# Index add: one plain transfer queue in a hand-written order, and gathers without repeated rows

## The chip, the cores and the metric

The kernel runs on one core of a Trainium2 chip. The core has a TensorE for matrix products (PE in the profile, its weight loads PEld), VectorE (DVE), ScalarE (ACT), GpSimd (POOL) and SyncE (SP), each with its own instruction stream, and 16 DMA engines that move data between the device memory and the core's SBUF. SP and ACT issue plain transfers here, each on a queue of its own; GpSimd issues the indirect ones, whose rows are given by a list of row numbers. The metric is the time of one execution on the device in microseconds; lower is better.

## The reference

`x` holds 32 batches of 512 rows of 256 floats (16.8 MB). For every batch there are 128 row numbers and 128 source rows, and each source row is added to the row of the result that its number names. Numbers can repeat within a batch, and then all their source rows are added.

```python
batch, seq, dim = 32, 512, 256
num_updates = 128
...
result = x.copy()
for b in range(batch):
    for i in range(num_updates):
        result[b, indices[b, i]] += source[b, i]
```

The inputs are the same at each execution. Each batch has between 107 and 119 distinct numbers among its 128.

## The kernel before

The 32 batches are handled in two ways.

Batches 0 to 25 (`NB` of them) go by rows. A plain transfer copies the whole batch of 512 KB from `x` to `out` (L119). A gather (L278) fetches the 128 rows of `x` that the batch's numbers name into SBUF. In `scatter` (L288) PE multiplies a 128x128 matrix of zeros and ones, which says which updates of the batch share a row, with the source rows; DVE adds the gathered rows (`res`, L299); and an indirect transfer writes the sums to `out` (L302). The scatter of a batch must come after its copy, since it overwrites rows of it. Where a number repeats, every update of that row holds the same complete sum, and only the first is written: `target` holds the row number, raised by `ROWS` for every later repeat, and the scatter's bound drops rows past `ROWS - 1`.

The matrix and `target` come from `equality` (L185), for four batches at a time: small matmuls spread the row numbers (L191), and DVE compares (`eq`, L199), masks (`early`, L206), reduces (`again`, L210) and forms `target` (L218). Groups are formed inside the loop, at its every fourth step.

Batches 26 to 31 (`N_FULL` of them) go whole: a plain transfer loads 512 KB into SBUF (L96), `compute_full` (L230) adds the source rows by matmuls with one-hot matrices (L243, L250), and a plain transfer stores the result (L259).

What sets the order: SP issues the index load and then the 26 copies, in order. ACT issues the 8 source loads of four batches each (L86) interleaved with the six whole loads, then the whole stores, the first three in the loop and the last three at its end (`STORES_LAST`). GpSimd's order is written out by hand with `pool_next`: five gathers ahead (`AHEAD`), then gather `b + 5` and scatter `b` in turn. On DVE and PE a scheduler places the instructions. It also gives each transfer its completion semaphore, and it derives the waits from the tiles. `ordered` declares which writes to `out` need no order among them, and ties each scatter to its copy.

Of the kernel before, what the change touches and what calls it, by code (L numbers as in the profile page):

```python
# [8 lines left out]

G = 4  # L10
N_FULL = 6
AHEAD = 5
COPY_RUN = 8192
FULL_AT = {1: 0, 4: 1, 8: 2, 12: 3, 16: 4, 20: 5}
STORES_LAST = 3


@with_exitstack
def kernel(
# [7 lines left out]
    nc = tc.nc  # L27

    B, S, D = x.shape
    _, NU = indices.shape  # L30
    assert NU == P and B % G == 0 and S % P == 0
    NG = B // G
    ROWS = B * S
    CH = S // P
    NB = B - N_FULL
# [11 lines left out]
    spool = ctx.enter_context(tc.tile_pool(name="spool", bufs=NG))  # L47
    xpool = ctx.enter_context(tc.tile_pool(name="xpool", bufs=N_FULL))
    hpool = ctx.enter_context(tc.tile_pool(name="hpool", bufs=2))
    epool = ctx.enter_context(tc.tile_pool(name="epool", bufs=3))  # L50
    mpool = ctx.enter_context(tc.tile_pool(name="mpool", bufs=2))
    gpool = ctx.enter_context(tc.tile_pool(name="gpool", bufs=AHEAD + 3))
    rpool = ctx.enter_context(tc.tile_pool(name="rpool", bufs=8))
    bpsum = ctx.enter_context(tc.tile_pool(name="bpsum", bufs=2, space=PSUM))
    apsum = ctx.enter_context(tc.tile_pool(name="apsum", bufs=3, space=PSUM))
# [3 lines left out]
    x_rows = x.rearrange("b s d -> (b s) d")  # L59
# [6 lines left out]

    writes = []

    def ordered(ins, after=()):
        for other in writes:  # L70
            if not any(other is a for a in after):
                tc.declare_no_dep(ins.ins, other.ins, reason="other rows")
        for a in after:
            tc.add_manual_dep(ins.ins, a.ins.name, SYNC, reason="the same rows")
        writes.append(ins)
        return ins


    idx_raw = const.tile([B, NU * 2], i32)
    nc.sync.dma_start(out=idx_raw[:, :], in_=indices.bitcast(i32))  # L80

    src = {}

    def load_src(g):
        t = spool.tile([P, G, D], f32, tag="src")
        nc.scalar.dma_start(  # L86
            out=t[:, :, :],
            in_=source[g * G : (g + 1) * G].rearrange("e u d -> u e d"),
        )
        src[g] = t  # L90

    full = {}

    def load_full(b):
        t = xpool.tile([P, CH, D], f32, tag="full")
        nc.scalar.dma_start(  # L96
            out=t[:, :, :], in_=x[b].rearrange("(j c) d -> j c d", c=CH)
        )
        full[b] = t

    load_src(0)
    load_full(NB)
    load_src(NB // G)
    load_full(NB + 1)
    load_src(1)
    g_next = 2
    for b in range(NB + 2, B):
        if b // G not in src:
            load_src(b // G)
        load_full(b)  # L110
        if g_next not in src:
            load_src(g_next)
        g_next += 1
    for g in range(NG):
        if g not in src:
            load_src(g)

    copies = [
        ordered(nc.sync.dma_start(out=out[b], in_=x[b], max_dma_last_dim=COPY_RUN))  # L119
        for b in range(NB)  # L120
    ]


    ident = const.tile([B, B], f32)
# [2 lines left out]
        out=ident[:, :],  # L127
        in_=ident[:, :],
# [13 lines left out]
        out=lower[:, :, :],  # L142
        in_=lower[:, :, :],
# [15 lines left out]
        out=idx_bt[:, :],  # L159
        in_=idx_raw[:, :].rearrange("b (u w) -> b u w", w=2)[:, :, 0],  # L160
# [5 lines left out]
    row_i = const.tile([P, B], i32)  # L166
    nc.vector.tensor_tensor(  # L167
        out=row_i[:, :], in0=base_i[:, :], in1=idx_f[:, :], op=Alu.add
# [3 lines left out]
        out=row_f[:, :], in0=base_i[:, :], in1=idx_f[:, :], op=Alu.add  # L172
# [10 lines left out]
    eqs, targets = {}, {}  # L183

    def equality(g):  # L185
        n = min(G, NB - g * G)
        sl = slice(g * G, g * G + n)
        rep = bpsum.tile([P, G, P], f32, tag="rep")
        for e in range(n):
            b = g * G + e  # L190
            nc.tensor.matmul(  # L191
                out=rep[:, e, :],
                lhsT=ident_h[:, b : b + 1].to_broadcast([B, P]),
                rhs=idx_h[:, :],
                start=True,
                stop=True,
            )
        eq = epool.tile([P, G, P], f32, tag="eq")
        nc.vector.tensor_tensor(  # L199
            out=eq[:, :n, :],  # L200
            in0=rep[:, :n, :],
            in1=idx_f[:, sl].unsqueeze(2).to_broadcast([P, n, P]),
            op=Alu.is_equal,
        )
        early = mpool.tile([P, G, P], f32, tag="early")
        nc.vector.tensor_tensor(  # L206
            out=early[:, :n, :], in0=eq[:, :n, :], in1=lower[:, :n, :], op=Alu.mult
        )
        again = mpool.tile([P, G], f32, tag="again")
        nc.vector.tensor_reduce(  # L210
            out=again[:, :n],
            in_=early[:, :n, :],
            axis=mybir.AxisListType.X,
            op=Alu.max,
        )

        target = epool.tile([P, G], i32, tag="target")
        nc.vector.scalar_tensor_tensor(  # L218
            out=target[:, :n],
            in0=again[:, :n],  # L220
            scalar=float(ROWS),
            in1=row_f[:, sl],
            op0=Alu.mult,
            op1=Alu.add,
        )
        eqs[g] = eq
        targets[g] = target


    def compute_full(b):  # L230
        x_tile = full[b]
        onehot = hpool.tile([P, CH, P], f32, tag="onehot")
        nc.vector.tensor_scalar(  # L233
            out=onehot[:, :, :],
            in0=line_f[:, :, :],
            scalar1=idx_f[:, b : b + 1],
            scalar2=None,
            op0=Alu.is_equal,
        )
        for c0 in range(0, CH, 2):  # L240
            ps = fpsum.tile([P, 2, D], f32, tag="ps")
            for k in range(2):
                nc.tensor.matmul(  # L243
                    out=ps[:, k, :],
                    lhsT=onehot[:, c0 + k, :],
                    rhs=src[b // G][:, b % G, :],
                    start=True,
                    stop=True,
                )
            nc.vector.tensor_tensor(  # L250
                out=x_tile[:, c0 : c0 + 2, :],
                in0=x_tile[:, c0 : c0 + 2, :],
                in1=ps[:, :, :],
                op=Alu.add,
            )

    def store_full(b):
        ordered(
            nc.scalar.dma_start(  # L259
                out=out[b].rearrange("(j c) d -> j c d", c=CH), in_=full[b][:, :, :]  # L260
            )
        )


    rows = {}
    on_pool, last_gather = [], [None]
# [1 line left out]
    def pool_next(ins):  # L268

        if on_pool:  # L270
            tc.add_manual_dep(
                ins.ins, on_pool[-1].ins.name, NOSYNC, reason="Pool's order"
            )
        on_pool.append(ins)

    def gather(b):
        t = gpool.tile([P, D], f32, tag="row")
        ins = nc.gpsimd.indirect_dma_start(  # L278
            out=t[:, :],
            out_offset=None,  # L280
            in_=x_rows,
            in_offset=bass.IndirectOffsetOnAxis(ap=row_i[:, b : b + 1], axis=0),
        )
        rows[b] = t
        last_gather[0] = ins
        pool_next(ins)

    def scatter(b):  # L288
        g, e = divmod(b, G)
        acc = apsum.tile([P, D], f32, tag="acc")  # L290
        nc.tensor.matmul(  # L291
            out=acc[:, :],
            lhsT=eqs[g][:, e, :],
            rhs=src[g][:, e, :],
            start=True,
            stop=True,
        )
        res = rpool.tile([P, D], f32, tag="res")
        nc.vector.tensor_tensor(  # L299
            out=res[:, :], in0=acc[:, :], in1=rows.pop(b)[:, :], op=Alu.add  # L300
        )
        ins = nc.gpsimd.indirect_dma_start(  # L302
            out=out_rows,
            out_offset=bass.IndirectOffsetOnAxis(ap=targets[g][:, e : e + 1], axis=0),
            in_=res[:, :],
            in_offset=None,
            bounds_check=ROWS - 1,
            oob_is_err=False,
        )
        ordered(ins, [copies[b]])  # L310
        if on_pool[-1] is last_gather[0]:
            pool_next(ins)

    for b in range(AHEAD):
        gather(b)
    for b in range(NB):
        if b + AHEAD < NB:
            gather(b + AHEAD)
        if b % G == 0:
            equality(b // G)  # L320
        scatter(b)
        if b in FULL_AT:
            compute_full(NB + FULL_AT[b])
            if FULL_AT[b] < N_FULL - STORES_LAST:
                store_full(NB + FULL_AT[b])
    for b in range(B - STORES_LAST, B):
        store_full(b)


# [28 lines left out]
```

## Time and profile before

| | us |
|---|---|
| median of three runs | 91.35 |
| the three runs | 90.51, 91.35, 92.36 |
| the profiled execution's own time | 91.25 |
| its span, first to last instruction | 89.5 |
| GpSimd busy | 54.2 |
| PE busy | 41.6 |
| DVE busy | 34.6 |

Busy time says how long an engine's instructions ran, not whether the kernel waited for them. The profile lists the DMA queues apart: for each one its packets, its bytes, and the time that the packets took as a share of the 16 engines' span. A strip gives the bytes per second in 40 equal slices of the span. Where the profile names what an idle engine waited for, the name is inferred from semaphore events; a wait for several things is put down to the one that came last by the profile.

### The profile page before, as it was taken

How to read it: one execution, taken by the hardware profiler on the slowest of the kernel's cores; microseconds unless marked ns; L12 is line 12 of the kernel's file. 1: busy time of each engine (PE TensorE's matmuls, PEld its weight loads, DVE VectorE, ACT ScalarE, POOL GpSimd, SP SyncE). 2: the span in 40 equal slices, each digit the busy share in tenths (PEclk: the TensorE clock that was granted, in tenths of full speed). 3: DMA queues.
4: the chain of work that ended last, by engine and by line, in shares of the span. 5: the costliest groups of instructions: out<-in, count | busy, mean ns of one | idle time of the engine just before them, and what ended most of it. 6: DMA issues, size and time to landing. Idle time of an engine off the chain costs nothing.

```text
span 89.5 us, 597 instructions
## 1 busy us (share of the span) xinstructions
PE 41.6 (46%) x127; PEld 26.2 (29%) x127; DVE 34.6 (39%) x79; POOL 54.2 (61%) x62
## 2 busy tenths in 40 slices
PE   0383008999649926893593550513557105500000
PEld 0260006767436803561381330210225002200000
DVE  0395020479746155934949191110113011022000
POOL 7277787647774317350058777877877787787500
PEclk9999999999985999669669995555555555555555
DMA  1999999999999999999999999899998999963210
GB/s 19 336 404 381 416 416 377 348 409 389 398 396 378 430 378 408 378 424 414 423 421 419 398 346 300 314 408 430 412 367 326 376 401 374 383 242 128 68 36 0
DMA packets 10579, 30.61 MB, mean 342 GB/s; under 512 B 1584, under 2 KB 5721, under 8 KB 8912
## 3 DMA queue, kind: packets, MB, share of 16 engines
q1 hardware_dynamic: 2128, 13.67, 39.0%
q10 hardware_dynamic: 5952, 10.49, 31.5%
q0 software_dynamic: 2496, 6.42, 19.5%
q8 instruction: 1, 0.02, 0.1%
q14 instruction: 2, 0.02, 0.0%
HBM read 24.41 MB, written 20.19 MB: 498 GB/s over the span
## 4 chain that ended last, share of the span: by engine, by line
DMA 50%; POOL 19%; issue 15%; POOLq 5%; DVE 3%; SPq 1%; PE 0%; DVEq 0%
DMA t<-in_x_dram,row_i 23%; DMA out_dram<-t 16%; POOL out_dram L302 11%; DMA out_dram<-in_x_dram 8%; POOL t L278 8%; POOLq L302 3%; DMA idx_raw<-in_indices_dram 3%; POOLq L353 1%; DVE t L250 1%; SPq L119 1%; DVE eq L199 1%; PE idx_ps L163 0%; DVE idx_bt L158 0%; DVE idx_f L165 0%; DVE row_i L167 0%
## 5 line engine op out<-in xcount | busy, mean ns | idle before, releaser
L302 POOL DMA_INDIRECT out_dram<-res,target x26 | 26.6, 1023 | 20.0 <-issue 8.3
L291 PE MATMUL acc<-t,eq 128*128 128x256 f32 x52 | 23.5, 576 | 23.2 <-DVE res L299 12.1
L278 POOL DMA_INDIRECT t<-in_x_dram,row_i x26 | 25.4, 978 | 9.5 <-issue 7.0
L299 DVE TENSOR_TENSOR res<-acc,t 128x256 f32<-128x256 f32 x26 | 10.9, 423 | 35.9 <-DMA t<-in_x_dram,row_i 26.5
L291 PEld LDWEIGHTS acc<-t,eq 128*128 128x128 f32 x52 | 12.4, 270 | 31.6 <-DVE res L299 14.7
L243 PE MATMUL ps<-t,onehot 128*128 128x256 f32 x48 | 16.2, 494 | 8.8 <-issue 6.3
L243 PEld LDWEIGHTS ps<-t,onehot 128*128 128x128 f32 x48 | 11.7, 255 | 13.1 <-issue 10.9
L250 DVE TENSOR_TENSOR t<-t,ps 128x512 f32<-128x512 f32 x12 | 8.1, 682 | 4.2 <-issue 3.2
L199 DVE TENSOR_TENSOR eq<-rep,idx_f 128x512 f32<-128x512 f32 (+1 forms) x7 | 4.5, 645 | 0.1
L206 DVE TENSOR_TENSOR early<-eq,lower 128x512 f32<-128x512 f32 (+1 forms) x7 | 4.5, 646 | 0.0
L210 DVE TENSOR_REDUCE again<-early 128x4 f32<-128x512 f32 (+1 forms) x7 | 4.5, 640 | 0.0
L191 PE MATMUL rep<-idx_h,ident_h 32*128 32x128 f16 x26 | 3.1, 258 | 0.0
L233 DVE TENSOR_SCALAR onehot<-line_f,idx_f 128x512 f32<-128x512 f32 x6 | 2.9, 486 | 0.0
L191 PEld LDWEIGHTS <-ident_h 32*128 32x128 f16 x26 | 1.9, 111 | 2.1 <-issue 2.0
L218 DVE SCALAR_TENSOR_TENSOR target<-again,row_f 128x4 int32<-128x4 f32 (+1 forms) x7 | 1.1, 154 | 3.5 <-issue 2.0
L163 PE MATMUL idx_ps<-ident,idx_bt 32*128 32x32 f32 x1 | 0.3, 281 | 3.8 <-DVE idx_bt L158 3.8
L158 DVE CAST idx_bt<-idx_raw 32x128 f32<-32x128 int32 x1 | 0.2, 215 | 3.4 <-DMA idx_raw<-in_indices_dram 3.4
L163 PEld LDWEIGHTS idx_ps<-ident,idx_bt 32*128 32x128 f32 x1 | 0.2, 176 | 3.7 <-POOL lower L141 3.7
L141 POOL TENSOR_SCALAR_AFFINE_SELECT lower<-lower 128x512 f32<-128x512 f32 x1 | 0.6, 627 | 0.0
L152 POOL IOTA line_i<- 128x512 int32 x1 | 0.6, 559 | 0.0
L140 POOL MEMSET lower<- 128x512 f32 x1 | 0.5, 515 | 0.0
L181 DVE CAST line_f<-line_i 128x512 f32<-128x512 int32 x1 | 0.4, 418 | 0.0
(12 smaller groups left out, 1.8 us busy)
## 6 DMA issues: line engine op xcount, KB each, us to landing
out_dram<-in_x_dram SPq DMA_DIRECT2D x26, 512.0 KB
t<-in_source_dram ACTq DMA_DIRECT2D x8, 512.0 KB
t<-in_x_dram ACTq DMA_DIRECT2D x6, 512.0 KB
out_dram<-t ACTq DMA_DIRECT2D x6, 512.0 KB
t<-in_x_dram,row_i POOLq DMA_INDIRECT x26
out_dram<-res,target POOLq DMA_INDIRECT x26
idx_raw<-in_indices_dram SPq DMA_DIRECT2D x1, 32.0 KB
```

Of the source, the lines that this page charges most:

```text
L191: nc.tensor.matmul(out=rep[:, e, :], lhsT=ident_h[:, b : b + 1].to_broadcast([B, P]), rhs=idx_h[:, :], start=True, stop=True,)
L199: nc.vector.tensor_tensor(out=eq[:, :n, :], in0=rep[:, :n, :], in1=idx_f[:, sl].unsqueeze(2).to_broadcast([P, n, P]), op=Alu.is_equal,)
L206: nc.vector.tensor_tensor(out=early[:, :n, :], in0=eq[:, :n, :], in1=lower[:, :n, :], op=Alu.mult)
L210: nc.vector.tensor_reduce(out=again[:, :n], in_=early[:, :n, :], axis=mybir.AxisListType.X, op=Alu.max,)
L218: nc.vector.scalar_tensor_tensor(out=target[:, :n], in0=again[:, :n], scalar=float(ROWS), in1=row_f[:, sl], op0=Alu.mult, op1=Alu.add,)
L233: nc.vector.tensor_scalar(out=onehot[:, :, :], in0=line_f[:, :, :], scalar1=idx_f[:, b : b + 1], scalar2=None, op0=Alu.is_equal,)
L243: nc.tensor.matmul(out=ps[:, k, :], lhsT=onehot[:, c0 + k, :], rhs=src[b // G][:, b % G, :], start=True, stop=True,)
L250: nc.vector.tensor_tensor(out=x_tile[:, c0 : c0 + 2, :], in0=x_tile[:, c0 : c0 + 2, :], in1=ps[:, :, :], op=Alu.add,)
L278: ins = nc.gpsimd.indirect_dma_start(out=t[:, :], out_offset=None, in_=x_rows, in_offset=bass.IndirectOffsetOnAxis(ap=row_i[:, b : b + 1], ...
L291: nc.tensor.matmul(out=acc[:, :], lhsT=eqs[g][:, e, :], rhs=src[g][:, e, :], start=True, stop=True,)
L299: nc.vector.tensor_tensor(out=res[:, :], in0=acc[:, :], in1=rows.pop(b)[:, :], op=Alu.add)
L302: ins = nc.gpsimd.indirect_dma_start(out=out_rows, out_offset=bass.IndirectOffsetOnAxis(ap=targets[g][:, e : e + 1], axis=0), in_=res[:, : ...
```

## The change

All plain transfers are issued by SP. Their order is a table: `s` is a source load, `f` a whole load, `c` a copy, `w` a whole store, and the entries of a step are issued ahead of the step's gather and scatter. Ahead of the loop stand `s0 c0 c1 s1 c2`; five of the six whole stores stand behind the loop. The whole batches are computed in the order 28, 29, 30, 31, 26, 27, at other steps than before. Gathers run four ahead instead of five. The first eight gathers read all 128 rows; from batch 8 on, a gather takes its row numbers from `target` with a bound, so that it leaves out the repeated rows. Their places in the tile keep older data, and the scatter drops the same places. For that, `equality` runs two groups ahead, and its tiles have four buffers instead of three. The tiles of the gathers have eight buffers as before. `ordered` no longer declares that a plain write is independent of another plain write, only pairs with an indirect one.

```diff
-AHEAD = 5
+AHEAD = 4
+RAW = 8
...
-FULL_AT = {1: 0, 4: 1, 8: 2, 12: 3, 16: 4, 20: 5}
-STORES_LAST = 3
+PLAN = {
+    0: "c3 s7 f28 c4",
+    1: "s2 c5",
+    2: "c6 f29",
+    3: "c7",
+    4: "c8 s3",
+    5: "c9 f30",
+    6: "c10",
+    7: "c11",
+    8: "s4 c12",
+    9: "c13 f31",
+    10: "c14",
+    11: "c15 s5",
+    12: "c16",
+    13: "c17 s6",
+    14: "c18 f26",
+    15: "c19 w28",
+    16: "c20",
+    17: "c21 f27",
+    18: "c22",
+    19: "c23",
+    20: "c24 c25",
+}
+LAST = "w29 w30 w31 w26 w27"
+FULL_AT = {3: 28, 6: 29, 9: 30, 13: 31, 18: 26, 21: 27}
...
-    epool = ctx.enter_context(tc.tile_pool(name="epool", bufs=3))
+    epool = ctx.enter_context(tc.tile_pool(name="epool", bufs=4))
...
+    def transfers(plan):
+        for what in plan.split():
+            kind, n = what[0], int(what[1:])
+            {"s": load_src, "f": load_full, "c": copy, "w": store_full}[kind](n)
...
     def gather(b):
         t = gpool.tile([P, D], f32, tag="row")
+        if b < RAW:
...
+        else:
+            g, e = divmod(b, G)
+            ins = nc.gpsimd.indirect_dma_start(
+                out=t[:, :],
+                out_offset=None,
+                in_=x_rows,
+                in_offset=bass.IndirectOffsetOnAxis(
+                    ap=targets[g][:, e : e + 1], axis=0
+                ),
+                bounds_check=ROWS - 1,
+                oob_is_err=False,
+            )
...
+    transfers("s0 c0 c1 s1 c2")
+    equality(0)
+    equality(1)
     for b in range(AHEAD):
         gather(b)
     for b in range(NB):
+        if b in PLAN:
+            transfers(PLAN[b])
         if b + AHEAD < NB:
             gather(b + AHEAD)
-        if b % G == 0:
-            equality(b // G)
+        if b % G == 0 and (b // G + 2) * G < NB:
+            equality(b // G + 2)
         scatter(b)
         if b in FULL_AT:
-            compute_full(NB + FULL_AT[b])
-            if FULL_AT[b] < N_FULL - STORES_LAST:
-                store_full(NB + FULL_AT[b])
-    for b in range(B - STORES_LAST, B):
-        store_full(b)
+            compute_full(FULL_AT[b])
+    transfers(LAST)
```

`load_src`, `load_full` and `store_full` issue with `nc.sync` instead of `nc.scalar`; nothing else in them changes, and `copy` is the former list of copies, one at a time.

More of the change, by code (lines that the diff above doesn't have):

```diff
@@ L49 @@
     hpool = ctx.enter_context(tc.tile_pool(name="hpool", bufs=2))
-    epool = ctx.enter_context(tc.tile_pool(name="epool", bufs=3))
+    epool = ctx.enter_context(tc.tile_pool(name="epool", bufs=4))
     mpool = ctx.enter_context(tc.tile_pool(name="mpool", bufs=2))
-    gpool = ctx.enter_context(tc.tile_pool(name="gpool", bufs=AHEAD + 3))
+    gpool = ctx.enter_context(tc.tile_pool(name="gpool", bufs=RAW))
     rpool = ctx.enter_context(tc.tile_pool(name="rpool", bufs=8))
@@ L67, with ordered @@
     writes = []
-    def ordered(ins, after=()):
-        for other in writes:
-            if not any(other is a for a in after):
+    def ordered(ins, after=(), indexed=False):
+        for other, other_indexed in writes:
+            if (indexed or other_indexed) and not any(other is a for a in after):
                 tc.declare_no_dep(ins.ins, other.ins, reason="other rows")
@@ L74, in ordered @@
             tc.add_manual_dep(ins.ins, a.ins.name, SYNC, reason="the same rows")
-        writes.append(ins)
+        writes.append((ins, indexed))
         return ins
@@ L80 @@
     nc.sync.dma_start(out=idx_raw[:, :], in_=indices.bitcast(i32))
-    src = {}
+    src, full, copies = {}, {}, {}
     def load_src(g):
         t = spool.tile([P, G, D], f32, tag="src")
-        nc.scalar.dma_start(
+        nc.sync.dma_start(
             out=t[:, :, :],
@@ L90, in load_src @@
         src[g] = t
-    full = {}
     def load_full(b):
         t = xpool.tile([P, CH, D], f32, tag="full")
-        nc.scalar.dma_start(
+        nc.sync.dma_start(
             out=t[:, :, :], in_=x[b].rearrange("(j c) d -> j c d", c=CH)
@@ L99, in load_full, with copy, store_full @@
         full[b] = t
[L101 to L121, printed above, removed]
+    def copy(b):
+        copies[b] = ordered(
+            nc.sync.dma_start(out=out[b], in_=x[b], max_dma_last_dim=COPY_RUN)
+        )
+    def store_full(b):
+        ordered(
+            nc.sync.dma_start(
+                out=out[b].rearrange("(j c) d -> j c d", c=CH), in_=full[b][:, :, :]
+            )
+        )
+    def transfers(plan):
+        for what in plan.split():
+            kind, n = what[0], int(what[1:])
+            {"s": load_src, "f": load_full, "c": copy, "w": store_full}[kind](n)
     ident = const.tile([B, B], f32)
@@ L255, in compute_full @@
             )
[L257 to L262, printed above, removed]
     rows = {}
@@ L277, in gather @@
         t = gpool.tile([P, D], f32, tag="row")
[L278 to L283, printed above, removed]
+        if b < RAW:
[3 more added lines that the diff above has]
+                in_=x_rows,
+                in_offset=bass.IndirectOffsetOnAxis(ap=row_i[:, b : b + 1], axis=0),
+            )
+        else:
+            g, e = divmod(b, G)
+            ins = nc.gpsimd.indirect_dma_start(
+                out=t[:, :],
+                out_offset=None,
+                in_=x_rows,
+                in_offset=bass.IndirectOffsetOnAxis(
[3 more added lines that the diff above has]
+                oob_is_err=False,
+            )
         rows[b] = t
@@ L309, in scatter @@
         )
-        ordered(ins, [copies[b]])
+        ordered(ins, [copies[b]], indexed=True)
         if on_pool[-1] is last_gather[0]:
             pool_next(ins)
+    transfers("s0 c0 c1 s1 c2")
+    equality(0)
+    equality(1)
     for b in range(AHEAD):
```

## The prediction

> **What bounds the kernel now.** I read the page's slices and queues first, then stages, then GpSimd's own order of work, then SP's waits.
>
> ```profile
> span 89.5 us, 597 instructions
> ...
> GB/s 19 336 404 381 416 416 377 348 409 389 398 396 378 430 378 408 378 424 414 423 421 419 398 346 300 314 408 430 412 367 326 376 401 374 383 242 128 68 36 0
> DMA packets 10579, 30.61 MB, mean 342 GB/s; under 512 B 1584, under 2 KB 5721, under 8 KB 8912
> ## 3 DMA queue, kind: packets, MB, share of 16 engines
> q1 hardware_dynamic: 2128, 13.67, 39.0%
> q10 hardware_dynamic: 5952, 10.49, 31.5%
> q0 software_dynamic: 2496, 6.42, 19.5%
> ...
> HBM read 24.41 MB, written 20.19 MB: 498 GB/s over the span
> ```
>
> q1 is SP's queue (copies), q10 ACT's (sources, whole loads and stores), q0 GpSimd's (gathers, scatters). Together they keep 16 DMA engines busy for 39.0 + 31.5 + 19.5 = 90% of 89.5, 80.6 us. No compute engine is near that. The idle tenth lies at the two ends, as the stages show (columns: busy us of PE, PEld, DVE, POOL, clock, DMA share, GB/s):
>
> ```profile
> 0.00:5.00 5.00, 1.23 (x9) 0.94 (x9) 1.34 (x7) 2.42 (x11) 1.00 0.60 202
> ...
> 80.00:85.00 5.00, 0.00 (x0) 0.00 (x0) 0.85 (x2) 3.52 (x4) 0.50 0.28 98
> 85.00:89.50 4.50, 0.00 (x0) 0.00 (x0) 0.00 (x0) 0.00 (x0) 0.50 0.08 26
> ```
>
> After 80 the DMA engines have 0.28 and then 0.08 of their time filled, yet the kernel isn't done. GpSimd is why. Its timeline (start, duration, operation, idle time before):
>
> ```profile
> 4.80 1.12 POOL L278 DMA_INDIRECT t<-in_x_dram,row_i  x1 [1.93 <-DVE row_f L171]
> ...
> 12.49 1.03 POOL L302 DMA_INDIRECT out_dram<-res,target  x1 [0.30 <-issue]
> ...
> 33.33 1.02 POOL L302 DMA_INDIRECT out_dram<-res,target  x1 [3.34 <-DVE res L299]
> 34.65 0.98 POOL L278 DMA_INDIRECT t<-in_x_dram,row_i  x1 [0.30 <-issue]
> 37.29 1.02 POOL L302 DMA_INDIRECT out_dram<-res,target  x1 [1.67 <-DVE onehot L233]
> 38.62 0.98 POOL L278 DMA_INDIRECT t<-in_x_dram,row_i  x1 [0.30 <-issue]
> 45.41 1.02 POOL L302 DMA_INDIRECT out_dram<-res,target  x1 [5.82 <-DVE eq L199]
> ...
> 83.45 0.99 POOL L302 DMA_INDIRECT out_dram<-res,target  x1 [0.30 <-issue]
> ```
>
> The scatter at 45.41 is number 8. From there GpSimd has 29 more indirect transfers to start and starts them without a gap: (83.45 - 45.41) / 29 = 1.31 us a slot. So everything after 45 is fixed by when scatter 8 could start; the engine named beside its 5.82 us had long been done, so I look for a transfer. SP's own waits tell which:
>
> ```profile
> SPq L119 <- DMA out_dram<-t: 8.3, 1, 8.3
> SPq L119 <- DMA t<-in_source_dram: 8.0, 3, 3.1
> ...
> SPq L119 <- DMA t<-in_x_dram: 1.0, 1, 1.0
> ```
>
> L119 issues copies, which need nothing from a source, a whole load or a store; still SP waits 17.3 us for such transfers to land before it may issue the next copy. I infer that plain transfers of both queues share a few completion semaphores, so a copy waits for an older transfer of ACT's. Copies come late, scatter 8 with them, and GpSimd pays at the end.
>
> **The change part by part.**
>
> *One plain queue.* 8 + 6 loads and 6 stores move from ACT to SP; ACT issues nothing.
>
> ```profile
> L86 ACTq DMA_DIRECT2D t<-in_source_dram x8: 374/413/1292, 0.8 to 27.7; - x8
> L96 ACTq DMA_DIRECT2D t<-in_x_dram x6: 529/1214/3782, 1.3 to 22.9; - x6
> L259 ACTq DMA_DIRECT2D out_dram<-t x6: 338/347/1542, 28.1 to 53.7; - x6
> ...
> L119 SPq DMA_DIRECT2D out_dram<-in_x_dram x26: 511/592/1078, 1.3 to 68.9; - x26
> ```
>
> By medians SP issues 8 x 0.41 + 6 x 1.21 + 6 x 0.35 + 26 x 0.59 = 28 us of work, spread over 75: nothing waits for it but transfers, and SP stays ahead as long as waits are for older transfers of its own order. I cost issue at nothing; its cover is the transfers already queued. The waits of the last fence become harmless: what is waited for stands earlier in the same queue. The first store (batch 28) sits after copy 19 while its sums are formed after scatter 3, so I put no stall there; if one came, every copy behind it would be late, and a scatter with each. The last store, batch 27's, has nothing behind it: its load is transfer 37 of 46, its own place is 46, and the sums between take DVE and PE a few matmuls.
>
> *Copies in step with scatters.* In the written order copy 25 is plain transfer 41 of 46. That removes the 3.34, 1.67 and 5.82 us of GpSimd's stalls. Its floor then: scatter 0 still at about 12.4 (its gather landed only then, see below), five gathers instead of six ahead of it, so 46 slots of 1.31 follow: last scatter starts at 72.7. What is late next is the DMA engines, below.
>
> *Gathers four ahead.* A gather then has four pairs of slots, 4 x 2.6 = 10.4 us, to land; the chain of waits shows 7.21 under load:
>
> ```profile
> 67.84 7.21 DMA t<-in_x_dram,row_i
> ```
>
> So nothing in the middle; at the start GpSimd idles one slot (1.3 us) before scatter 0, hidden because the DMA engines set the end.
>
> *Repeated rows left out.* In the drawn indices batches 8 to 25 repeat 257 of their 2,304 rows: 257 KB, 0.26 of q0's 6.42 MB; at 17.5 us for q0 that is 0.7 us of DMA work saved. Price on GpSimd: these gathers take a bound like the scatters,
>
> ```profile
> L302 POOL DMA_INDIRECT out_dram<-res,target x26 | 26.6, 1023 | 20.0 <-issue 8.3
> L278 POOL DMA_INDIRECT t<-in_x_dram,row_i x26 | 25.4, 978 | 9.5 <-issue 7.0
> ```
>
> 18 x (1023 - 978) ns = 0.8 us at most, nothing at least; last scatter then at 73.5 and still covered. They also wait for target (L218) instead of row_i. Behind a gather that waits stands the scatter of its step, and DVE's res waits for the gather. But target is formed at least one whole group, four pairs of slots, ahead of its first gather: it would have to be some 10 us late. Three groups now come ahead of the first res:
>
> ```profile
> L199 DVE TENSOR_TENSOR eq<-rep,idx_f 128x512 f32<-128x512 f32 (+1 forms) x7 | 4.5, 645 | 0.1
> L206 DVE TENSOR_TENSOR early<-eq,lower 128x512 f32<-128x512 f32 (+1 forms) x7 | 4.5, 646 | 0.0
> L210 DVE TENSOR_REDUCE again<-early 128x4 f32<-128x512 f32 (+1 forms) x7 | 4.5, 640 | 0.0
> ...
> 4.67 0.69 DVE L199 TENSOR_TENSOR eq<-rep,idx_f 128x512 f32<-128x512 f32 x1
> ...
> 11.67 0.42 DVE L299 TENSOR_TENSOR res<-acc,t 128x256 f32<-128x256 f32 x1 [3.72 <-DMA t<-in_x_dram,row_i]
> ```
>
> 3 x (0.65 + 0.65 + 0.64) = 5.8 us from 4.67 end at 10.5, before 11.67: free.
>
> *Whole batches' sums.* DVE and PE work in order, so a whole load that is late holds back the next res. Each of these loads stands in the queue right behind the copy of its own step or one source later (copy 18 is transfer 31, load 26 is 32; copy 21 is 36, load 27 is 37), and the next scatter needs the copy behind it anyway: no added wait, at most the 2 us of one more transfer.
>
> *Stores last.* Five stores, 2.6 MB, follow copy 25 and keep the engines filled while the last scatters go out, where now they idle.
>
> *The sum.* With the stalls gone the engines' bytes set the end, so I need the rate. Transfers of the stages 5 to 50, 60 to 80, 50 to 60 and 60 to 65:
>
> ```profile
> DMA packets 7192, 18.01 MB, mean 400 GB/s; under 512 B 842, under 2 KB 4431, under 8 KB 6423
> ...
> DMA packets 1732, 7.51 MB, mean 375 GB/s; under 512 B 472, under 2 KB 476, under 8 KB 1124
> ...
> DMA packets 718, 3.47 MB, mean 347 GB/s; under 512 B 148, under 2 KB 148, under 8 KB 430
> ...
> DMA packets 495, 2.10 MB, mean 421 GB/s; under 512 B 129, under 2 KB 131, under 8 KB 339
> ```
>
> Mixed with loads the engines move 400 GB/s; once copies and indirect transfers are nearly alone, 375, between 347 and 421. On one queue a copy's packets always meet only indirect ones, so copies and indirect bytes go at 375, sources and whole batches at 400. The first 5 us move 202 x 5 = 1.01 MB, as now, half of it source, half copies. Left: (10.49 - 0.52) / 0.400 = 24.9 us, and (13.67 - 0.49 + 6.42 - 0.26) / 0.375 = 51.6 us. Last landing: 5.0 + 24.9 + 51.6 = 81.5. Copy 25 lands near 75, so scatter 25 starts near 76 and can land by 81.5; at the 7.21 above it would be 83.3, up to 1.8 more. From the last landing to the end of the span I keep today's time: the DMA strip of 80 to 89.5 (40 slices of 0.2375) ends after slice 23,
>
> ```profile
> DMA  7121392000860005800009300000000000000000
> ```
>
> that is at 85.5, so 4.0 us. Span 85.5. The profiled execution took 91.25 for a span of 89.5, 1.75 around it: 87.3 us. That execution stands 0.1 under the median of 91.35.
>
> A rule would forbid this: the Trainium skill, "HBM Reference", section "Specifications (TRN2)", gives a core about 358 GB/s of HBM. With the 44.3 MB that remain to be read and written that makes an estimate of 124 us, already over today's span. The trace disagrees, with its 498 GB/s over the span, so I keep the rates of the rows.
>
> **The rivals.**
> (a) *The single queue is slower.* Copies no longer overlap another plain queue, and everything runs at the 347 of 50 to 60. Then 29.3 MB / 0.347 = 84.6 us, span 93.6, 95.3 us: slower. For it: the strip falls to 300, 314 and 326 (slices 24, 25 and 30), where plain transfers are nearly all copies. Against it: 60 to 65 has as little of q10 and reaches 421. The loss passes 2% (93.2 us) below 358 GB/s, break-even is at 366.
> (b) *GpSimd still sets the end.* Stalls of about 11 us come back, from copies queued behind sources and loads or from DVE held by a late whole load; last scatter again at 83.5, 91 us: no change. Up to 4 us of stall is free (73.5 + 4 + a landing of 2 to 4). Against it: copy 8 is now the 15th plain transfer, about 7.9 MB, landed before 30 at these rates, where it is needed at 33.
> (c) *The engines hold 421*, as in 60 to 65, since nothing runs dry: 29.3 / 0.421 = 69.7, last landing 74.7 if GpSimd didn't need 73.5 + 1 + 2 = 76.5; span 80.5, 82.3 us.
>
> **How the numbers follow.** Forecast 0.52, (a) 0.18, (b) 0.18, (c) 0.12. About 2% is what a measurement of this kernel can tell from no change: 89.5 and 93.2 are the edges. Faster: nearly all of the forecast's case and (c), 0.62. Slower: the lower part of (a), 0.11. Within 2%: (b), the rest of (a) and the forecast's slow end, 0.27. Range: 400 GB/s throughout gives 5.0 + 73.3 + 4.0 + 1.75 = 84.1, so from 84.4; up to 92.0, a rate of 363 or a case (b) with its end one slot late. The forecast's own range is 85.0 to 89.5.
>
> **What would show it.** Right: GpSimd's idle time between 27 and 46 falls from 11 us to under 4; SP waits only for transfers of its own queue; DMA share near 1 from 5 to 80 and whole stores among the last landings; q0 carries 6.16 MB; the rate from 5 to the last landing is 382. Wrong: a mean rate under 370 with full engines is (a); a last scatter starting after 80 with engines half idle is (b); an SP wait for DVE or PE ahead of a store, or res waiting on a target, breaks the parts that I cost at nothing.

## The result, and the profile after

| | us |
|---|---|
| changed kernel, median of four runs | 87.03 (86.51 to 87.52) |
| kernel before, beside it, median of four | 91.85 (90.51 to 92.69) |
| ratio | 0.957, 95% interval 0.944 to 0.970 |
| the profiled execution and its span | 86.76, 85.0 |
| predicted | 87.3 (84.4 to 92.0) |

The change takes 4 to 5 us off. Medians here and below take all executions, while the ratios leave out those over 1.5% above the fastest of their kernel. The time is within 0.3 us of the forecast, but that is luck: the profile shows that three of the forecast's terms were wrong, and that the errors cancelled.

The page of the changed kernel, slices and queues:

```profile
span 85.0 us, 609 instructions
...
GB/s 15 297 324 304 392 390 399 419 411 419 414 430 396 422 414 421 401 418 409 420 400 425 397 403 428 404 421 417 419 431 409 414 416 416 387 205 69 55 133 114
...
q1 hardware_dynamic: 8080, 24.15, 71.8%
q0 software_dynamic: 2496, 6.16, 18.4%
...
HBM read 24.41 MB, written 20.19 MB: 525 GB/s over the span
```

One plain queue carries 24.15 MB, and the indirect queue 6.16, as the change says. After the first five slices the strip has no slice under 387 until the bytes run out; before, it fell to 346, 300, 314 and 326. Then come five thin slices at the end. By stages (the last number is GB/s, the one before it the engines' share):

```profile
0.00:5.00 5.00, 1.56 (x12) 1.33 (x13) 2.30 (x9) 3.10 (x11) 1.00 0.55 184
5.00:10.00 5.00, 4.12 (x17) 2.65 (x15) 4.34 (x10) 3.78 (x5) 1.00 0.99 331
...
5.00:75.00 70.00, 41.49 (x117) 27.48 (x115) 30.63 (x69) 50.24 (x50) 0.78 1.02 406
...
75.00:85.00 10.00, 0.00 (x0) 0.00 (x0) 1.80 (x3) 2.32 (x3) 0.54 0.26 103
```

From 5 to 75 the engines are full and move 406 GB/s, where I had put 382. In the last 10 us they are three quarters empty, and the kernel waits. SP's waits, and the issue rows of the whole stores (duration minimum, median, maximum; first and last start):

```profile
SPq L132 <- DVE t L269: 10.4, 1, 10.4
SPq L127 <- DMA out_dram<-in_x_dram: 4.2, 4, 1.2
```

```profile
L132 SPq DMA_DIRECT2D out_dram<-t x6: 332/340/370, 45.6 to 81.4; - x6
```

Copies (L127) now wait 4.2 us for older copies and 1.1 us for a source load, all of their own queue. (This trace lacks many semaphore events, so these totals may be too low; the second trace below has the landing of every plain transfer.) But the last whole store, batch 27's, stands 10.4 us at the head of SP and is issued at 81.4, when the engines have been nearly idle for 5 us. It waits for its sums on DVE (start, duration, operation, idle time before):

```profile
73.94 0.42 DVE L325 TENSOR_TENSOR res<-acc,t 128x256 f32<-128x256 f32 x1 [1.69 <-DMA out_dram<-res,target]
76.70 0.42 DVE L325 TENSOR_TENSOR res<-acc,t 128x256 f32<-128x256 f32 x1 [2.34 <-issue]
79.27 0.69 DVE L269 TENSOR_TENSOR t<-t,ps 128x512 f32<-128x512 f32 x1 [2.15 <-remote]
80.68 0.69 DVE L269 TENSOR_TENSOR t<-t,ps 128x512 f32<-128x512 f32 x1 [0.71 <-remote]
```

Two things delay them. The scheduler has put them behind the last `res` of the loop, which waits for the last gathered rows, as the chain of what ended last shows (start, duration):

```profile
70.43 4.62 DMA t<-in_x_dram,target
75.05 1.60 DVEq L325
76.65 0.04 issue
76.70 0.06 DVE res L325
76.76 2.49 another core or an unknown queue
```

And "remote" names a release for which the profile finds no instruction that ended just before. Batch 27's load was issued at 50.6, and in the second trace below the same load takes 12.4 us to land, so what is left for the sums to wait for is PE's matmuls. Those stand in PE's timeline from 69.97, with a modelled end at 71.96, 7.3 us before DVE may begin:

```profile
69.97 1.99 PE L262 MATMUL ps<-t,onehot 128*128 128x256 f32 x8
```

The drains with which the engines end show the same from the other side (duration minimum, median, maximum; first and last start):

```profile
L381 POOLq DRAIN  x3: 40/108/5540, 77.2 to 84.7; - x3
...
L381 PEldq DRAIN  x2: 13/5066/10120, 70.6 to 84.6; - x2
```

PE's drain begins at 70.6 and takes 10.1 us, to 80.7, just when DVE's last wait ends. So PE's work was reported done late, later than its rows say. I call this a late end of PE. There is one more, at 40.17, where `eq` waits 5.5 us; it reaches GpSimd:

```profile
42.12 1.01 POOL L328 DMA_INDIRECT out_dram<-res,target  x1 [2.82 <-DVE res L325]
...
47.92 1.01 POOL L328 DMA_INDIRECT out_dram<-res,target  x1 [0.81 <-issue]
...
77.40 0.98 POOL L328 DMA_INDIRECT out_dram<-res,target  x1 [0.76 <-DVE res L325]
```

Of GpSimd's 11 us of stalls between 27 and 46 only the first of these, 2.8 us, is left (the 0.3 us ahead of every one of its transfers not counted). Scatter 8 starts at 34.3 instead of 45.4, the last one at 77.4 instead of 83.45.

### The profile page after: what moved, and what is told of

Same layout as the page of the kernel before. It is cut to its first block, busy times and chain, and to the rows that moved or that the text cites. A ratio compares the mean times of both kernels' runs of the same rounds, so it can differ in the third digit from the quotient of the medians.

```text
span 85.0 us, 609 instructions
## 1 busy us (share of the span) xinstructions
PE 43.0 (51%) x127; PEld 28.8 (34%) x127; DVE 34.7 (41%) x79; POOL 55.7 (65%) x62
## 2 busy tenths in 40 slices
DMA packets 10579, 30.34 MB, mean 357 GB/s; under 512 B 1584, under 2 KB 5725, under 8 KB 8912
## 3 DMA queue, kind: packets, MB, share of 16 engines
q1 hardware_dynamic: 8080, 24.15, 71.8%
q0 software_dynamic: 2496, 6.16, 18.4%
## 4 chain that ended last, share of the span: by engine, by line
DMA 35%; POOL 25%; issue 23%; another core or an unknown queue 4%; POOLq 3%; DVE 3%; DVEq 2%; PE 0%
DMA out_dram<-res,target 20%; DMA t<-in_x_dram,target 13%; POOL out_dram L328 10%; POOL t L291 7%; POOL t L300 7%; POOLq L328 3%; DMA idx_raw<-in_indices_dram 2%; DVEq L325 2%; DVE t L269 2%; DVE idx_bt L177 1%; PE idx_ps L182 0%; DVE idx_f L184 0%; DVE row_i L186 0%; POOLq L300 0%
## 5 line engine op out<-in xcount | busy, mean ns | idle before, releaser
L317 PE MATMUL acc<-t,eq 128*128 128x256 f32 x52 | 22.3, 568 | 10.6 <-DVE res L325 5.6
L262 PE MATMUL ps<-t,onehot 128*128 128x256 f32 x48 | 18.4, 551 | 10.0 <-DVE t L269 8.5
L300 POOL DMA_INDIRECT t<-in_x_dram,target x18 | 18.7, 1041 | 5.5 <-issue 4.9
L317 PEld LDWEIGHTS acc<-t,eq 128*128 128x128 f32 x52 | 12.9, 275 | 18.3 <-issue 8.4
L262 PEld LDWEIGHTS ps<-t,onehot 128*128 128x128 f32 x48 | 13.3, 286 | 14.1 <-issue 10.9
L291 POOL DMA_INDIRECT t<-in_x_dram,row_i x8 | 8.3, 1040 | 3.4 <-issue 2.1
L210 PE MATMUL rep<-idx_h,ident_h 32*128 32x128 f16 x26 | 3.6, 303 | 5.2 <-DVE res L325 4.9
L210 PEld LDWEIGHTS <-ident_h 32*128 32x128 f16 x26 | 2.4, 132 | 7.3 <-DVE res L325 6.1
```

The source lines that it names most:

```text
L210: nc.tensor.matmul(out=rep[:, e, :], lhsT=ident_h[:, b : b + 1].to_broadcast([B, P]), rhs=idx_h[:, :], start=True, stop=True,)
L262: nc.tensor.matmul(out=ps[:, k, :], lhsT=onehot[:, c0 + k, :], rhs=src[b // G][:, b % G, :], start=True, stop=True,)
L291: ins = nc.gpsimd.indirect_dma_start(out=t[:, :], out_offset=None, in_=x_rows, in_offset=bass.IndirectOffsetOnAxis(ap=row_i[:, b : b + 1], ...
L300: ins = nc.gpsimd.indirect_dma_start(out=t[:, :], out_offset=None, in_=x_rows, in_offset=bass.IndirectOffsetOnAxis(ap=targets[g][:, e : e ...
L317: nc.tensor.matmul(out=acc[:, :], lhsT=eqs[g][:, e, :], rhs=src[g][:, e, :], start=True, stop=True,)
```

## The experiments

All compare with the kernel before, run beside them. They ran in three groups, each on a chip of its own; a difference of a few per cent is read within a group only.

### First group: the queue and the place of the last stores

**The changed kernel again**, one execution.

> The changed kernel once more, for a second trace. Theory (the end is batch 27's store, held by DVE's order): SP again waits some 10 us for DVE before the last store, which is issued after 79; the DMA engines are under 0.5 busy between 76 and 82; span 84.5 to 86. Rival (that wait was one execution's accident): the last store is issued before 76 and the span is under 83.

83.35 us, span 81.6: the rival's outcome, not mine. The same program was 3.4 us faster than in its first profile, and the trace says where: SP's wait for the sums, the sums in DVE's timeline, and the drains.

```profile
SPq L132 <- DVE t L269: 8.7, 2, 7.6
```

```profile
73.51 0.42 DVE L325 TENSOR_TENSOR res<-acc,t 128x256 f32<-128x256 f32 x1 [2.43 <-DMA t<-in_x_dram,target]
73.86 1.27 DVE L269 TENSOR_TENSOR t<-t,ps 128x512 f32<-128x512 f32 x2
```

```profile
L381 POOLq DRAIN  x3: 40/108/6848, 74.0 to 81.4; - x3
...
L381 PEldq DRAIN  x2: 13/726/1440, 67.1 to 81.2; - x2
```

Here PE's drain takes 1.4 us, DVE has no "remote" wait at all, and the two sums follow the last `res` without a pause. The last store is issued at 75.2 and lands at 79.5, the last scatter starts at 74.2 instead of 77.4. The rates are nearly the same (404 GB/s from 5 to 50 and 417 from 50 to 75, against 402 and 412). The last store is issued 6.2 us sooner: the last `res` is 3.2 us sooner, with the stalls behind `eq` gone, and the sums' own waits of 2.9 us are gone too. So these two traces put the first profile's 3.4 us down to the late ends of PE, not to the written order. Copies wait 22.1 us here, all for older transfers of their own queue:

```profile
SPq L127 <- DMA out_dram<-in_x_dram: 13.6, 13, 1.4
SPq L127 <- DMA t<-in_source_dram: 6.4, 4, 2.8
...
SPq L127 <- DMA t<-in_x_dram: 2.1, 2, 1.1
```

**The kernel before again**, one execution.

> The kernel before once more, for a second trace. Theory (copies held by ACT's transfers make scatter 8 late, and GpSimd then runs without a gap to the end): a stall of 4 us or more ahead of a scatter between 38 and 50, then slots of 1.31 us to about 84. On the rate: if the 366 GB/s between 50 and 80 belongs to the order of the transfers, this trace has 355 to 378 there too; if it was an accident of one execution, 395 or more.

90.29 us, span 88.6. The slow stretches recur (slices 22, 23 and 30):

```profile
GB/s 18 310 419 377 400 420 378 355 394 401 396 404 369 414 386 417 373 418 414 430 431 407 264 292 439 409 372 409 418 400 297 339 390 418 390 374 169 83 26 0
```

They belong to the old order and aren't a chance of one execution: from 50 to 80 the rate is 373 GB/s, within the 355 to 378 that I expected for that. Scatter 8 starts at 44.65, after a stall of 4.83 us. This trace has the landing of every plain transfer, and in it copies wait 52.2 us, not 17.3, for transfers that ACT issued:

```profile
SPq L119 <- DMA t<-in_source_dram: 22.2, 6, 6.0
SPq L119 <- DMA out_dram<-t: 20.1, 4, 8.4
...
SPq L119 <- DMA t<-in_x_dram: 9.9, 2, 8.2
```

DVE has no "remote" wait here either.

**Two queues in the written order**: loads and whole stores go back to ACT, each at its place in the table, copies stay on SP.

```diff
 # in load_src, load_full and store_full
-nc.sync.dma_start(
+nc.scalar.dma_start(
```

> The changed kernel with sources, whole loads and whole stores issued by ACT again, in the same written order, copies by SP. Theory (what was gained is the order, in which a transfer waits only for older ones of the same list, and not the number of queues): time 86 to 88.5. Rival (a single queue is what gives the rate, by keeping copies from running beside another plain queue): 89.5 to 92.

91.06 us (90.55 to 92.28), ratio 1.005 (0.999 to 1.011): the whole gain is gone, and my theory with it; the time is the rival's. SP's waits and the strip:

```profile
SPq L127 <- DMA t<-in_x_dram: 27.3, 6, 7.8
SPq L127 <- DMA out_dram<-t: 18.3, 4, 7.5
...
SPq L127 <- DMA t<-in_source_dram: 6.2, 2, 3.7
```

```profile
GB/s 22 326 361 354 408 418 402 401 385 422 423 384 390 403 394 427 413 409 427 420 419 388 359 260 282 428 415 419 424 353 290 323 409 421 399 271 113 74 31 0
```

Copies wait 52 us for transfers that ACT issued, as in the kernel before, though the table, the gathers and the computation are those of the changed kernel. The trace also says what they wait for. The plain transfers of both queues share eight completion semaphores, and each of the eight is used by SP and by ACT. In each of the 12 waits of a copy, here and in the second trace of the kernel before, the copy waits for the semaphore that it will itself use, until the transfer of ACT that had it before has landed. One of these is a load that ACT issued at 2.4 and that landed at 16.2. So copies come late and then in a bunch, and the dips are those of before, 260 and 290. Two queues with semaphores of their own were not tried, so that a second queue must cost anything isn't shown. Both losses return together: scatter 8 starts at 39.0, the last at 82.7.

**Whole loads earlier**: loads and sums of batches 26 and 27 (and source 6) come two to four steps sooner, so that no store should have to wait.

```diff
-    11: "c15 s5",
+    11: "s6 f26 c15 s5",
-    13: "c17 s6",
-    14: "c18 f26",
+    13: "f27 c17",
+    14: "c18",
-    17: "c21 f27",
+    17: "c21",
-FULL_AT = {3: 28, 6: 29, 9: 30, 13: 31, 18: 26, 21: 27}
+FULL_AT = {3: 28, 6: 29, 9: 30, 13: 31, 15: 26, 18: 27}
```

> The changed kernel with the loads and sums of batches 26 and 27 two to four steps earlier (source 6 with them), stores at the same places. Theory (the end of the changed kernel is batch 27's store, issued at 81.4 though its load landed at 62): the last store is issued by 72, the engines stay full to about 77, scatter 25 lands last near 79; span 81 to 83.5, time 82.5 to 85.5. Rival (the engines' bytes set the end, as the prediction had it): time 86.5 to 87.5 as before the edit.

84.67 us (84.37 to 84.92), ratio 0.934 (0.925 to 0.943). The time is what the theory gave. The last store is issued at 67.1, and no store waits over 1.5 us. What ends the kernel then is GpSimd:

```profile
L381 POOLq DRAIN  x3: 40/107/7732, 74.2 to 82.5; - x3
```

The last scatter starts at 74.46 and lands at 79.34, and the drain behind it ends only at about 82.0. But 84.67 is no less than the single 83.35 of the unmoved kernel on this chip. Whether moving the sums gains anything needs both on one chip, in rounds; the third group does that.

### Second group: other orders, and the repeated rows

**The changed kernel, in rounds.**

> The changed kernel timed beside the edits of it on one chip. Two executions so far gave 86.76 us (two late releases by PE: 5.5 us ahead of eq and 2.2 us ahead of batch 27's sums) and 83.35 us (none). Theory (the late releases are a matter of the execution or of the chip, not of the program): 83 to 84.5 without them, 86 to 87.5 with them, and the trace shows them exactly where the time is over 86. Rival (they follow from the order of the instructions and the first look was the odd one): 86 to 87.5 in most rounds.

87.14 us (86.42 to 89.34), ratio 0.959 (0.952 to 0.966), the first result again. Its trace has late ends of PE, with 16.5 us of waits behind them:

```profile
DVE onehot L252 <- remote: 9.4, 1, 9.4
DVE res L325 <- remote: 5.4, 2, 3.7
DVE t L269 <- remote: 1.7, 2, 1.0
```

**Both queues by turns**: the same list of transfers, every second one on ACT.

```diff
+    turn = [0]
+    def queue():
+        turn[0] += 1
+        return nc.sync if turn[0] % 2 else nc.scalar
 # in all four functions that start a plain transfer
-nc.sync.dma_start(
+queue().dma_start(
```

> The changed kernel with its list of plain transfers dealt out in turn to SP and ACT, so that there are two plain queues but the written order holds to within one transfer. Theory (what counts is that copies keep coming in the written proportion and no queue runs dry): within 1 us of the changed kernel on this chip, 82.5 to 85 (or 86 to 87.5 where that one is slow). Rival (two plain queues cost rate, or a copy waits for the other queue's transfers again): 89 to 92, as with sources, whole loads and stores on ACT.

91.72 us (91.12 to 91.80), ratio 1.010 (1.002 to 1.019): the rival's time. The rate is nearly kept (401 GB/s from 5 to 50, 390 from 50 to 75), but the order isn't. SP's longest waits ahead of a transfer, and GpSimd's longest wait for a copy:

```profile
SPq L132 <- DMA t<-in_source_dram: 14.8, 3, 9.0
```

```profile
POOL out_dram L333 <- DMA out_dram<-in_x_dram: 7.1, 1, 7.1
```

One queue runs ahead of the other: when SP issues the 29th transfer of the list, at 47.4 after the wait of 9.0 us, ACT has already issued three that stand behind it in the list, the last of them at 42.7. A copy lands only at about 73, by the profile, and its scatter holds GpSimd, whose order is written out, for 7.1 us. The Trainium skill, "DMA: Bandwidth & Descriptors", section "Issuing engines are not separate DMA queues", says that starting transfers on several engines saves only the time to start them. By that, I would have the placing make little difference. This case disagrees: 87.14 on one queue, 91.72 by turns on the same chip. What the second queue costs here is time that SP waits before it may start a transfer.

**Loads first**: one queue, but all 14 loads, then the 26 copies in a row, then the six stores.

```diff
-PLAN = {
...
-}
-LAST = "w29 w30 w31 w26 w27"
+PLAN = {}
+LAST = "w28 w29 w30 w31 w26 w27"
...
-    transfers("s0 c0 c1 s1 c2")
+    transfers("s0 f26 s6 f27 s1 s7 f28 s2 f29 s3 f30 s4 f31 s5")
+    transfers(" ".join(f"c{b}" for b in range(NB)))
```

> The changed kernel, still on one queue, with all sources and whole loads first, then the 26 copies, then the six stores. Theory (GpSimd's start is set by copy 0, now plain transfer 15, landing near 24; 46 slots of 1.31 us follow the first scatter): last scatter starts at 85 to 87, time 90.5 to 93. On the rate: rival 1 (copies beside indirect transfers alone are slow) 340 to 378 GB/s between 30 and 55; rival 2 (the dips belong to a queue that had run dry) 395 or more there.

100.75 us (99.94 to 101.42), ratio 1.112 (1.100 to 1.125), over 7 us longer than I expected. GpSimd's first scatter waits 17.5 us and starts at 28.2, 4 us later than I had put copy 0's landing; the 46 slots behind it take 64.5 us instead of 60.3, so the last scatter starts at 92.7; and the span ends 6.1 us after that. GpSimd's wait and the strip (a slice is 2.47 us):

```profile
POOL out_dram L306 <- DVE early L203: 17.5, 1, 17.5
```

```profile
GB/s 20 307 308 368 367 408 381 376 374 394 426 335 332 322 372 400 386 337 340 371 394 401 365 366 341 371 372 385 408 417 420 414 256 118 2 91 97 97 47 0
```

In slices 11 to 27 the loads are done and the stores stand behind the copies, so plain transfers are copies; the engines are full, and the mean of the 17 is 364 GB/s, as rival 1 had it. In the next four slices, where stores follow, it is 408 to 420. So a run of copies is slower than a mixture, on one queue too. Why, wasn't tried.

**All rows gathered**: no repeated row is left out.

```diff
-        if b < RAW:
+        if True:
```

> The changed kernel with every gather reading all 128 rows by row_i again. Theory (0.26 MB of gathers at about 0.41 MB per us, GpSimd 18 x 0.04 us shorter and not on the path): 0.3 to 1.0 us slower than the changed kernel on this chip. Rival (not the engines' bytes but the last store's issue sets the end): within 0.3 us.

87.14 us (84.39 to 89.59), the same median as the changed kernel beside it. The 0.26 MB bring nothing that can be measured, though the spread of these runs, 5 us, would hide the 0.7 us that I gave them; the fastest of them is even 2 us under the fastest of the changed kernel. On GpSimd a gather without a bound took 1.02 us here; with one it took 1.04 in the first profile, and so did the eight without a bound there. So the bound costs at most some 0.02 us.

### Third group: the end

**The changed kernel once more**, beside the next three.

> The changed kernel unaltered, on the chip on which the next three run, so that they have it beside them. If the last whole store waits for the sums of batch 27 (the theory), the last store is issued after 75 us while the engines empty at about 77, and the time is 83 to 87.5 us: near 83.5 where PE's releases come at its modelled ends, near 87 where DVE has idle waits of 2 us and more behind PE's matmuls. The rival, that the engines' bytes set the end, would have the DMA share near 1 up to 3 us before the end.

88.60 us (87.61 to 90.05), ratio 0.973 (0.960 to 0.985). Late ends of PE again, 14.2 us of waits in all, and the last store waits 9.6 us and is issued at 82.2.

**Whole loads earlier, beside it.**

> Whole loads of batches 26 and 27 and their sums two to four steps earlier, as in the run whole_early, now with the changed kernel on the same chip. The theory: the last store no longer waits for DVE, it is issued before 75 us, and the time is 84 to 85 us, at or below the changed kernel's, by 2 us and more where the changed kernel stands near 87. The rival, that chips differ and the placing of the sums does nothing: same time as the changed kernel within 0.5 us.

88.02 us (86.34 to 93.17), ratio 0.956 (0.940 to 0.971): 0.6 us under the changed kernel by the medians and some 1.5 us by the ratios, whose intervals overlap. That is neither the theory's 2 us and more nor clearly the rival's 0.5 us and less, so whether the placing of the sums gains anything isn't settled. The last store is issued at 67.9, so its wait did go, but the late ends are still there and hit another chain:

```profile
DVE onehot L252 <- remote: 4.8, 1, 4.8
DVE res L325 <- remote: 1.9, 1, 1.9
DVE eq L218 <- remote: 1.8, 1, 1.8
```

DVE's order feeds both the sums and the `res` of the scatters. With the sums out of the way the `res` are late: the last scatter starts at 78.5, 4.1 us later than the same kernel's in the first group.

**Seven whole batches**: batch 25 goes whole too, with the whole loads from step 8 on spread again.

```diff
-N_FULL = 6
+N_FULL = 7
...
-LAST = "w29 w30 w31 w26 w27"
+LAST = "w29 w30 w31 w26 w27 w25"
-FULL_AT = {3: 28, 6: 29, 9: 30, 13: 31, 18: 26, 21: 27}
+FULL_AT = {3: 28, 6: 29, 9: 30, 12: 31, 14: 26, 16: 27, 18: 25}
```

> Batch 25 goes whole as well (7 whole, 25 by rows), with the whole loads spread from step 8 on. If Pool's chain and its end set the time of whole_early (scatter 25 starts at 74.5, Pool's last drain ends 2.6 us behind the landing), two slots of about 1.3 us go: 2.0 to 2.6 us less than whole_early, 82 to 82.8 us. The rival, that the engines' bytes set it: one batch whole moves 0.26 MB more than by rows less its repeats, about 0.29 MB at 405 GB/s = 0.7 us more than whole_early, 85 to 85.5 us. A third: seven sums keep DVE and PE so busy that a store waits for them again, 86 us and more.

86.91 us (86.34 to 88.45), ratio 0.951 (0.938 to 0.963). It isn't near the 82 to 82.8 that two slots fewer on GpSimd would give. The third expectation came, a store that waits for DVE again (7.0 us), but that the sums are too many for DVE or PE isn't shown: the trace has one of the largest waits behind late ends of PE,

```profile
SPq L132 <- DVE res L325: 7.0, 1, 7.0
```

```profile
DVE onehot L252 <- remote: 15.6, 2, 9.7
```

and the last scatter starts at 78.6, no sooner than with six. Its median is 1.7 us under that of the changed kernel on this chip, but the intervals of the two ratios overlap. It is the best version in this group; that it beats the changed kernel isn't settled.

**Gathers five ahead.**

```diff
-AHEAD = 4
+AHEAD = 5
```

> Gathers five ahead of the scatters in place of four, nothing else. The theory says that the gathers' lead costs and brings nothing: within 0.6 us of the changed kernel on this chip. The rival: the scatters wait for their gathered rows, so one more gather ahead takes 1 us and more off Pool's chain, and if that sets the end off the time; or the first scatter, now behind five gathers, starts 1.3 us later and the time is 1 us longer.

88.66 us (88.49 to 91.74) against 88.60, ratio 0.970 (0.955 to 0.985): no difference.

### What the late ends of PE go with

The four profiles of the first group, of the kernel before and with one and two queues, have no "remote" wait on DVE; all eight of the second and third groups have 6 to 17 us of them, and so has the first profile of the changed kernel, 8.4 us. With three chips only, that looks like a matter of the chip or its condition and not of an order: the unmoved kernel is in each of the three groups. The kernel before has no trace on the second and third chip, so whether it has late ends there isn't known, and the chip of the first two profiles isn't on record.

The traces record when PE reported work as done. In the second trace of the changed kernel all 43 such events stand within 0.02 us of the modelled ends. In the first profile only 21 of the 43 are recorded. Of these, the event at 40.15 comes 6.1 us after the last modelled end before it, and the last two, at 79.25 and 80.65, come 8.2 and 8.7 us after the last two modelled ends; DVE goes on within 0.03 us of each of the three. In the run in rounds, four events come within 0.13 us of each other, from 46.90 to 47.03, although by the rows the last four ends before them lie 0.43 us apart, and DVE, which had waited 9.4 us, starts at 46.92. There, at least, several ends were held up and reported together. All nine profiles with late ends lack such events. That isn't the cause by itself, since the first profile of the kernel before lacks over half of them too, and has no late end.

What holds PE up isn't shown. The rows' granted clock doesn't tell: it is 0.795 in the first group's run of the changed kernel and 0.775 in the second's, but lower, 0.714 and 0.726, in the first group's runs with two queues and of the kernel before, which have no late end. That the recording itself holds PE up is a rival that no run here can exclude. The Trainium skill, "TensorE: Matmul & The Clock Gate", section "Seeing it yourself", warns that records of PE's clock have been unreliable and that the clock has been seen stuck at a quarter. A clock slower than recorded could give late ends behind modelled ones, though hardly four ends within 0.13 us; no run here can show whether it is the cause of the others.

## Why the prediction was right, and which of its steps were not

**What bounds the kernel before** was read rightly. Copies that wait for ACT's transfers made scatter 8 late, and GpSimd paid at the end. In traces that have every landing, copies of the kernel before wait 52.2 us for ACT's transfers; with one queue they wait 22.1 us, for their own queue alone, and scatter 8 starts 11 us sooner; with loads on ACT again they wait 52 us for ACT's and the gain is gone. That the waits go by shared completion semaphores was an inference; the traces show it, as said above.

**GpSimd's floor** was 72.7 to 73.5 for the last scatter's start. Without late ends of PE it started at 74.2 (the kernel again, first group), with them at 77.4 to 78.9. Stalls between 27 and 46 fell from 11 us to under 4 (2.8 us in the first profile), as announced, and what was left came from DVE.

**The rate is the first step that failed.** "Copies and indirect bytes go at 375, sources and whole batches at 400" priced the copies by a stretch in which they ran nearly alone. Its premise, that on one queue a copy's packets meet only indirect ones, is shown by no run. The price of such a stretch was about right: 364 in the run with loads first. But the written order leaves no such stretch, and the whole mixture goes at 406. With the 0.92 MB of the first 5 us, (30.34 - 0.92) / 0.406 = 72.5 us puts the last landing at 77.5; I had 81.5. Rival (c), with 421, was nearer. Rival (a)'s 347 is near what copies in a row reach on one queue, but this order has no such row; its own arithmetic is a little off (29.3 / 0.347 is 84.4 us, its two edges lie at 356 and 364 GB/s, and the range's upper end at 361). The Trainium skill, "HBM Reference", does say under the same heading, "Specifications (TRN2)", that "A core streaming alone measures well above the per-core share". The 525 GB/s of this profile, read and written, agree; the 124 us went by the share for two busy cores.

**"The last store, batch 27's, has nothing behind it ... the sums between take DVE and PE a few matmuls" is the second.** Nothing stands behind it in the queue, but the end of the kernel does. Its sums stand behind the last `res` in DVE's order, which wait for gathers, and, in this profile, behind PE's late end. I had put "an SP wait for DVE or PE ahead of a store" among the signs of a failure, and it came: 10.4 us. It moved the last landing from the 77.5 that the bytes allow to 83.7. The wait in DVE's order alone, without late ends, is nearly free: the store lands at 79.5, when GpSimd is about to be done too.

**The tail is the third, smaller one.** I kept today's 4.0 us from the last landing to the end of the span; it was 1.3 (83.7 to 85.0). The 4.0 hold where a scatter lands last, since GpSimd's drain then runs on for 2.6 to 3.3 us; behind the plain store that landed last here the span ended after 1.3 us. So the sum reads 77.5 + 6.2 + 1.3 + 1.76 = 86.8, where I had 81.5 + 4.0 + 1.75 = 87.3: 4.0 us too much for the bytes and 2.7 for the tail, 6.2 too little for the store. That these nearly cancel is luck; the same program without late ends took 83.35 us, 4 us under the forecast and 1 us under its range.

**The small parts** held: issue on one engine cost nothing (in the first two traces copies wait only for older transfers of their own queue), gathers four or five ahead are the same, and 6.16 MB on the indirect queue against 6.42 can't be measured.

## What to carry to other kernels

When several transfer queues share the engines, and a later stage consumes what they bring in order, write one list and issue it from one queue, at least where the queues share completion semaphores as they do here: a queue of one's own for loads made the copies wait for them and cost the whole gain, although the same bytes moved. Compare waits only between traces that hold all their events. Price a stage by rows with the same mixture, not by the kind of transfer; and follow a last store back through every engine that forms its data, in that engine's order, before calling it free. Time a kernel whose end hangs on in-order engines on more than one chip, since the same kernel gained about 8% on one (by one execution) and 3% on another.

## What was not expected of the hardware

- PE's ends were reported up to 8.7 us later than its modelled rows. On two chips every trace has DVE waits of the kind (6 to 17 us in all), on one none. The drain of PE at the end shows it (10.1 us against 1.4 for the same program), and so does a DVE wait named "remote".
- Copies from device memory to device memory, in a row, run at 364 GB/s, with slices down to 322, on full engines; mixed with some loads or stores, one queue held 402 to 417.
- GpSimd's last drain goes on for 2.6 to 3.3 us after its last scatter has landed, which makes a scatter a dearer last transfer than a plain store (1.3 us).
- Plain transfers of SP and ACT share eight completion semaphores in this program, so that a copy on one queue waited up to 7.8 us for a load on the other.
- With the list dealt to two queues SP waited up to 9.0 us for one source load of 512 KB; with the same list on one queue the longest such wait was 1.1 us in the first profile and 2.8 in the second.
